# Two more feature tiles by seven products, norm 2's root begun earlier, and sums of operands moved to GpSimd

## The chip, the cores and the metric

One core of one Trainium2 chip runs the kernel. Its engines run side by side, each through its own queue in order: TensorE (PE, with PEld for its weight loads), VectorE (DVE), ScalarE (ACT), GpSimd (POOL) and SyncE (SP, which only issues transfers here). The metric is the device time of one execution in microseconds (us). The kernel before takes 871.9 us in the median of 3 runs (871.86 to 872.1). The page and the trace are of one execution of 871.7 us, whose span from the first to the last instruction is 869.9 us; the 1.8 us that lie around the span are taken as fixed.

## The reference

One layer of a decoder over 520 columns (512 positions of a prompt and 8 single samples) and 1024 features, in float32:

```python
xn = rmsnorm(x, norm1_g);  z = xn @ w_in                # pooling, recurrent, chunk branch and gates
x = x + (ga * (ya @ w_pa) + gb * (yb @ w_pb) + gc * (yc @ w_pc)) @ w_o
xn = rmsnorm(x, norm2_g)                                # norm 2
h = gelu(causal_dwconv(xn @ wg, cw, cb)) * (xn @ wu)    # 3072 features, 24 tiles of 128
x = x + h @ wd;  y = rmsnorm(x, final_norm_g)
```

All of the change but its part on constants lies in norm 2 and the three products of the gated mixer.

## The kernel before, in words

Features lie on the 128 partitions, the 520 columns along the free dimension, in two halves of 260. One "tile" of a product is 128 output features by 520 columns with 8 slices of 128 input features. Each float32 operand is split in two parts that TensorE takes: a high part (ScalarE copies and rounds it) and a low part (the difference). Each slice then costs three matmuls per half (high by high, high by low, low by high), so a plain tile of 8 slices is 48 matmuls of 128x260. Weights come by SyncE's queue as `raw` (a ring of 4), ScalarE makes `wh`, VectorE subtracts to get `wl` (`Chunk.low`), or, where `by_dma` is set, ScalarE writes the negated high part and GpSimd issues a transfer that adds the source to it (`low_by_dma`).

**Order.** Everything is written out once, in one order. `run_jobs` goes through the products; `now` counts tiles, and `after(n, fn)` runs `fn` when `now` has moved on by n tiles. So work of VectorE, ScalarE and GpSimd is interleaved with TensorE's by tile counts, and each engine's queue holds what is written in that order. An instruction that waits holds all that stands behind it on its engine.

**Stages.** After the last product of the first half, `w_o` (8 tiles, `wo_post` adds x, squares it and splits it into the operands `xg2`), the mixer's products come two tiles at a time: gate tiles m, m+1 (`wg`), two column blocks of the down product `wd` of the group of four before, then up tiles m, m+1 (`wu`), and two more blocks. Group p holds feature tiles 4p to 4p+3.

**Norm 2.** `rstd_small` sums the squares with five small matmuls (`n2p`), ScalarE takes the square root (behind the load of its table), VectorE and GpSimd build two diagonal tiles (`n2d`), and `rstd_bcast` spreads them over the partitions with four matmuls (`n2b`), two of each diagonal. Before, `g_post` calls the first behind gate tile 0 and the second behind gate tile 1. Plain tiles 0 to 3 are multiplied with the operands `xg2`, which lack the root; their results are scaled with it later (`fg_post`, `scaled`).

**Pairs.** From tile `MP` = 6 on, two tiles are made by seven products of half size (`Pair`, `run_pair`), each of 12 matmuls, instead of eight. They need seven operands `X0` to `X6`, made once by `operands()` from the four quarters of the scaled input (b11, b12, b21, b22: `rows`, 16 instructions) by sums and differences, each again as a high and a low part (`operand`). Their weights are sums of the raw weights (`Pair.sums`, four additions of 128x512 a pair) with their own high and low parts. `SEQ_PAIR` sets the order: product 0, a filler (half of a block of `wd`), products 3 and 2, the other half of that block, products 1, 4, 5, a filler, product 6, a filler. Tiles 4 and 5 (`MN` to `MP`) are plain, but on operands with the root (`plain`). `X0` is `X8` negated by GpSimd (`minus_first`).

**Rings.** Most tiles of 128x536 floats (`A(...)`) come from one ring of `NA` = 51; constants (`sts`, `wsT`, `bsb`, `wz`) have places of their own.

Of the kernel before, what the change touches and what calls it, by code (L numbers as in the profile page):

```python
# [16 lines left out]
P = 128  # L17
D = 1024
# [33 lines left out]
def trunk_kernel(ctx: ExitStack, tc: tile.TileContext, t: dict, o: dict):  # L52
# [35 lines left out]
    sts = const.tile([P, NSTATE], F32, name="sts")  # L88
    wsT = const.tile([P, 4, P], F32, name="wsT")
    bsb = const.tile([P, 4, P], F32, name="bsb")  # L90
# [11 lines left out]
    class Chunk:  # L102
# [5 lines left out]
        def load(self, parts=(0, None)):  # L108
            if not hasattr(self, "raw"):
                self.raw = wp.tile([P, self.size], F32, name="raw" + self.tag, bufs=2 if self.tag else RAW)  # L110
            q = slice(parts[0] * P, parts[1] * P if parts[1] else self.n)
            nc.sync.dma_start(self.raw[:, q], self.src[:, q])
# [271 lines left out]
    def constants():  # L384
        nc.sync.dma_start(sts, t["sts"])
        nc.sync.dma_start(wsT, t["wsT"])
        nc.sync.dma_start(bsb.rearrange("p g i -> p (g i)"), t["bs"].partition_broadcast(P))
# [245 lines left out]
    def pool_post(gi, ps):  # L633
# [178 lines left out]
    def wo_post(j, ps):  # L812
# [3 lines left out]
        st2[0] = square_add(st2[0], x1[j], f"x1q{j}")  # L816

# [9 lines left out]
    def fg_post(m, ps):  # L827
# [5 lines left out]
        if m < MN:  # L833
            v.tensor_mul(two(ext[:, 2:]), acc(ps), two(rs2[0]))
        else:
            s.activation(two(ext[:, 2:]), acc(ps), AF.Copy)
        fg_rest(m, ext)

    def fg_rest(m, ext):
# [13 lines left out]
        def scaled():  # L853
            if m < MN:
                v.tensor_mul(y, y, rs2[0])
# [11 lines left out]
    def half_rows(q):  # L867
        i, h = q
        bq[q] = [A(f"b{i}{h}_{n}") for n in range(2)]

# [23 lines left out]
    def plain(k):  # L894

        return [[two(xo[n][k % 4 // 2][e])[:, k % 2, :] for n in ((8, 7), (1, 5))[k // 4]] for e in range(2)]

    def diff(n, a, b):
        y = [A(f"d{n}{i}") for i in range(2)]
        for i in range(2):  # L900
            v.tensor_sub(y[i], a[i], b[i])
        return y

    def minus_first(i):
        hl = [A(f"X0{i}_{e}", F32R) for e in "hl"]
        for q, p in zip(hl, xo[8][i]):
            g.tensor_scalar(q, f(p), -1.0, None, op0=ALU.mult)
        xo.setdefault(0, []).append(hl)

    dd = {}  # L910

    def operands():
        for q in ((0, 0), (0, 1), (1, 0), (1, 1)):
            half_rows(q)
        steps = [lambda k=k: rows(k) for k in range(8)]
        steps += [lambda n=n, q=q: operand(n, bq[q]) for n, q in ((8, (0, 0)), (7, (0, 1)), (1, (1, 0)), (5, (1, 1)))]

        def d3():
            dd[3] = diff(3, bq[0, 0], bq[0, 1])

# [308 lines left out]
```

## Time and profile before

| | us |
|---|---|
| median of 3 runs | 871.9 |
| profiled execution, its span | 871.7, 869.9 |
| PE busy, share of the span | 856.5, 98% |
| DVE busy, share of the span | 591.3, 68% |
| ACT busy, share of the span | 444.6, 51% |
| POOL busy, share of the span | 128.1, 15% |

PE is the engine whose busy time fills the span. Matmuls are pipelined, so what one costs is read from how many start in a stretch and not from the mean of one. The mean granted TensorE clock is 0.995 of the full 2.4 GHz. Rows in order of time name the start, the length, the engine, the line of the kernel, the operation and its tiles as out<-in; in brackets stands how long the engine was idle before it, and what ended that.

### The profile page before, as it was taken

What the parts mean: (1) busy time and instruction counts of PE and PEld (TensorE: products, weight loads), DVE (VectorE), ACT (ScalarE), POOL (GpSimd) and SP (SyncE); (2) the same over time, 40 slices, a digit from 0 to 9 for tenths busy, and PEclk for the clock granted to TensorE, in tenths of its full rate; (3) what the DMA queues carried; (4) which work ended last, traced back from release to release, by engine and by line L of the source; (5) the groups of instructions that cost most, each with busy time, mean ns of one, the idle gap of its engine ahead of it and who ended that gap; (6) DMA issues with size and microseconds to landing.
All of it is one profiled execution on the core that took longest, in us unless ns stands there. A gap on an engine that the chain in (4) does not pass through costs nothing.

```text
span 869.9 us, 16887 instructions
## 1 busy us (share of the span) xinstructions
PE 856.5 (98%) x7142; PEld 852.7 (98%) x7142; DVE 591.3 (68%) x919; ACT 444.6 (51%) x652; POOL 128.1 (15%) x183
## 2 busy tenths in 40 slices
PE   8999999999999999999999999999999999999995
PEld 7999999999999999999999999999999999999994
DVE  5897989698875443135554797677777768778645
ACT  7555464578342343222335775556556556555642
POOL 0503411111100000020002114111110110111232
PEclk9999999999999999999999999999999999999997
DMA  9334233223233224342345975656545555555532
GB/s 291 130 116 128 65 100 97 75 86 95 76 94 102 76 95 121 98 158 87 122 139 168 209 165 125 157 110 150 134 111 155 135 122 146 122 151 133 145 97 99
DMA packets 36251, 108.40 MB, mean 125 GB/s; under 512 B 4152, under 2 KB 7352, under 8 KB 36152
## 3 DMA queue, kind: packets, MB, share of 16 engines
q1 hardware_dynamic: 25440, 83.08, 30.6%
q0 software_dynamic: 9216, 22.68, 14.1%
q10 hardware_dynamic: 1520, 1.57, 0.5%
q8 instruction: 56, 0.92, 0.4%
q14 instruction: 19, 0.16, 0.1%
HBM read 92.13 MB, written 15.57 MB: 124 GB/s over the span
## 4 chain that ended last, share of the span: by engine, by line
PE 97%; DVE 1%; ACT 1%; DMA 0%; SPq 0%; issue 0%; POOL 0%; DVEq 0%; POOLq 0%; ACTq 0%
PE pj L206 73%; PE pa L257 12%; PE c L257 6%; PE pf L257 3%; PE lru L206 1%; DMA x<-in_x 0%; PE vm L749 0%; PE po L206 0%; DVE bc L519 0%; DVE y L1051 0%; PE vt L742 0%; ACT L537 0%; PE n31p L452 0%; ACT n31d L461 0%; PE n30p L452 0%
## 5 line engine op out<-in xcount | busy, mean ns | idle before, releaser
L127 DVE TENSOR_TENSOR wl<-raw,wh 128x1024 fp32r<-128x1024 f32 (+1 forms) x108 | 126.4, 1176 | 36.8 <-ACT wh L118 36.7
L206 PE MATMUL pj<-xn_h,wh 128*128 128x260 f32 x704 | 141.9, 283 | 0.1
L206 PE MATMUL pj<-xn_l,wh 128*128 128x260 f32 x704 | 141.4, 282 | 0.0
L206 PE MATMUL pj<-xn_h,wl 128*128 128x260 f32 x704 | 140.8, 281 | 0.0
L118 ACT ACTIVATE wh<-raw 128x1024 fp32r<-128x1024 f32 (+1 forms) x118 | 117.7, 1005 | 4.4 <-DMA raw<-in_w_in 2.3
L206 PEld LDWEIGHTS pj<-xn_l,wh 128*128 128x128 f32 x704 | 108.7, 188 | 0.0
L206 PEld LDWEIGHTS pj<-xn_h,wh 128*128 128x128 f32 x704 | 108.1, 188 | 0.3 <-ACT r L537 0.3
L206 PEld LDWEIGHTS pj<-xn_h,wl 128*128 128x128 f32 x704 | 108.2, 188 | 0.0
L206 PE MATMUL pj<-h_l,wh 128*128 128x260 f32 x384 | 82.5, 282 | 0.6 <-DVE h_l L956 0.6
L206 PE MATMUL pj<-h_h,wh 128*128 128x260 f32 x384 | 82.4, 282 | 0.0
L206 PE MATMUL pj<-h_h,wl 128*128 128x260 f32 x384 | 82.3, 282 | 0.0
L1008 POOL DMA_DIRECT2D x1d<-dn x40 | 35.1, 877 | 263.7 <-ACT dn L1007 263.7
L206 PEld LDWEIGHTS pj<-h_l,wh 128*128 128x128 f32 x384 | 61.3, 188 | 0.8 <-DVE h_l L956 0.8
L206 PEld LDWEIGHTS pj<-h_h,wl 128*128 128x128 f32 x384 | 61.3, 188 | 0.0
L206 PEld LDWEIGHTS pj<-h_h,wh 128*128 128x128 f32 x384 | 61.1, 188 | 0.0
L690 ACT ACTIVATE gt<-pj 128x520 f32<-128x520 f32 x24 | 14.5, 606 | 81.3 <-PE pj L206 81.2
L187 DVE TENSOR_TENSOR wl<-sum,wh 128x1024 fp32r<-128x1024 f32 x36 | 43.9, 1220 | 0.9 <-ACT wh L184 0.9
L164 DVE TENSOR_TENSOR wl<-raw,wh 128x1024 fp32r<-128x1024 f32 x18 | 22.1, 1226 | 31.8 <-ACT wh L161 31.8
L184 ACT ACTIVATE wh<-sum 128x1024 fp32r<-128x1024 f32 x36 | 37.8, 1050 | 0.8 <-DVE sum L179 0.8
L848 DVE SCALAR_TENSOR_TENSOR fc<-fg,par,fc 128x512 f32<-128x512 f32 x48 | 36.0, 749 | 1.1 <-ACT fc L844 0.3
L955 ACT ACTIVATE h_h<-fc 128x520 fp32r<-128x520 f32 x24 | 15.4, 640 | 24.4 <-DVE fc L987 11.1
L1007 ACT ACTIVATE dn<-pj 128x520 f32<-128x520 f32 x40 | 23.9, 598 | 6.6 <-PE pj L206 5.0
(482 smaller groups left out, 2329.1 us busy)
## 6 DMA issues: line engine op xcount, KB each, us to landing
raw<-in_w_in SPq DMA_DIRECT2D x50, 512.0 KB, 3.6
raw<-in_wg SPq DMA_DIRECT2D x24, 512.0 KB, 4.0
raw<-in_wu SPq DMA_DIRECT2D x24, 512.0 KB, 3.9
raw<-in_wd SPq DMA_DIRECT2D x24, 512.0 KB, 5.3
x1d<-dn POOLq DMA_DIRECT2D x40, 260.0 KB, 4.4
raw<-in_w_pb SPq DMA_DIRECT2D x8, 512.0 KB, 3.6
raw<-in_w_o SPq DMA_DIRECT2D x8, 512.0 KB, 3.5
wl<-in_wu POOLq DMA_DIRECT2D x6, 512.0 KB, 8.2
```

The source lines that it names most:

```text
L118: s.activation(self.h[:, q], self.raw[:, q], AF.Copy)
L127: v.tensor_sub(self.l[:, q], self.raw[:, q], f(self.h[:, q]))
L164: v.tensor_sub(self.new("h1", "wl"), self.raw[1], f(self.W["h1", "wh"]))
L184: s.activation(self.new(n, "wh"), self.s[n], AF.Copy)
L187: v.tensor_sub(self.new(n, "wl"), self.s[n], f(self.W[n, "wh"]))
L206: te.matmul(ps[:, h, :TH], ww, xx[h] if isinstance(xx, list) else xx[:, h * TH:(h + 1) * TH], start=first and n == 0, stop=last and n == 2)
L257: te.matmul(bank[b], ww, xx, start=seen[b] + j + e == 0, stop=i >= (6, 1, 5)[b] and j == 3 and e == 2, skip_group_check=True)
L690: s.activation(two(y), acc(ps), AF.Sigmoid)
L848: v.scalar_tensor_tensor(y[:, :SEQ], ext[:, r:r + SEQ], pc("fcw", r * MF + m), y[:, :SEQ], op0=ALU.mult, op1=ALU.add)
L955: after(0.25, lambda: s.activation(h, y, AF.Copy))
L1007: s.activation(two(y), acc(ps), AF.Copy)
L1008: nc.gpsimd.dma_start(x1d[:, j, :], y, accum_op=ALU.add)
```

## The change

- `MP` goes from 6 to 4 and `MN` is gone: tiles 4 and 5 become a pair, in `wg` and in `wu`. The low parts of all eight remaining plain tiles are made by transfer (`by_dma=True`); gate tiles 0 and 1 had theirs from VectorE.
- Norm 2's sums are written 0.75 tiles, its broadcast 1.25 tiles behind the end of `w_o` (`N2`), inside gate tiles 0 and 1; gate tile 1 is then scaled as its result leaves PSUM.
- `X0` is b11 itself. `X2` is negated instead (in `operand`, `sign=-1.0`), and `add_parts`, `wg_out` and `wu_out` take the signs into account. The sums and differences for the operands and the multiplication `scaled` go from VectorE to GpSimd (`g.tensor_sub`, `g.tensor_add`, `g.tensor_mul`). The steps are 0.3 tiles apart for the first eight, then 0.4.
- `sts` becomes four loads (`h0t`, `rcs`, `ffs`, `pls`); these but `h0t`, and `wsT`, `bsb`, `wz` and the small raw weights, move into the ring, which has 57 places.

```diff
     def constants():
-        nc.sync.dma_start(sts, t["sts"])
-        nc.sync.dma_start(wsT, t["wsT"])
...
+        for d, c in ((h0t, S_H), (rcs, S_RC), (ffs, S_FF), (pls, S_PL)):
+            nc.sync.dma_start(d, t["sts"][:, c:c + d.shape[1]])
+        nc.sync.dma_start(wsT, t["wsT"].rearrange("p g i -> p (g i)"))
...
         st2[0] = square_add(st2[0], x1[j], f"x1q{j}")
+        if j == 7:
+            after(N2[0], norm2)
+            after(N2[1], norm2_rows)
...
         def scaled():
-            if m < MN:
-                v.tensor_mul(y, y, rs2[0])
+            if m < MP:
+                g.tensor_mul(y, y, rs2[0])
...
+        def first_diff():
+            d3.extend(A(f"d{i}") for i in range(2))
+            onto(g.tensor_sub, d3, b11, b12)
+
         steps = [lambda k=k: rows(k) for k in range(8)]
...
+        steps += [lambda: operand(0, b11), first_diff, lambda: operand(3, d3),
+                  lambda: onto(g.tensor_sub, b12, b22, b12), lambda: operand(1, b21),
+                  lambda: onto(g.tensor_add, d3, d3, b22), lambda: operand(5, b22), lambda: operand(2, d3, -1.0),
+                  lambda: onto(g.tensor_sub, d3, d3, b21), lambda: operand(4, b12), lambda: operand(6, d3)]
         for i, fn in enumerate(steps):
-            after(XSTEP[0] * min(i, 12) + XSTEP[1] * max(0, i - 12), fn)
+            after(XSTEP[0] * min(i, 8) + XSTEP[1] * max(0, i - 8), fn)
...
+    def norm2():
+        n2[0] = rstd_small([st2[0]], D, "n2")
+
+    def norm2_rows():
+        rs2[0] = rstd_bcast(n2[0], "n2")
+        for i in range(8):
+            if i in held:
+                x = held.pop(i)
                 v.tensor_mul(x[:, 2:], x[:, 2:], rs2[0])
                 fg_rest(i, x)
-            after(0.25, operands)
+        after(0.25, operands)
...
+    def add_parts(n, o_, a, b):
+        if n == "c12":
+            v.scalar_tensor_tensor(o_, a, -1.0, b, op0=ALU.mult, op1=ALU.subtract)
+        else:
+            v.tensor_add(o_, a, b)
...
-NA, RAW, HS, LS, LOADS, HLEAD, LLEAD = 51, 4, 6, 6, 3, 3, 2
+NA, RAW, HS, LS, LOADS, HLEAD, LLEAD = 57, 4, 6, 6, 3, 3, 2
 NP = 6
-MN, MP = 4, 6
-XSTEP = (0.4, 0.4)
+MP = 4
+N2 = (0.75, 1.25)
+XSTEP = (0.3, 0.4)
```

Over the whole program TensorE's queue holds 7105 instructions before and 7081 now, VectorE's 921 and 928.

ScalarE around norm 2's root (`n` is the small tile with the mean squares and their root, `fg` a gate tile on its way to the convolution, `n2r` the broadcast root). Before:

```order
L99 ACTIVATE wl<-wh 128x1024
L831 ACTIVATE fg_5531<-pj 128x520
L467 ACT_TABLE_LOAD
L467 ACTIVATE n_5541<-n_5540 104x5
L118 ACTIVATE wh<-raw 128x1024
L99 ACTIVATE wl<-wh 128x1024
L831 ACTIVATE fg_5612<-pj 128x520
L489 ACTIVATE n2r<-n2b 128x520
```

Now:

```order
L98 ACTIVATE wl<-wh 128x1024
L471 ACT_TABLE_LOAD
L471 ACTIVATE n_5534<-n_5533 104x5
L838 ACTIVATE fg_5561<-pj 128x520
L117 ACTIVATE wh<-raw 128x1024
L98 ACTIVATE wl<-wh 128x1024
L493 ACTIVATE n2r<-n2b 128x520
```

The table and the root stand ahead of gate tile 0's copy, and gate tile 1's copy is gone. On TensorE, 24 matmuls stand between `n2p` and `n2b` now, and 48 before.

VectorE in the two plain tiles ahead of the first product of tiles 4 and 5 (`X..l` are low parts of operands, `fc` an activated gate tile, `h_l` a low part for the down product). Before, from tile 3's scaling with the root to its product with its up tile (`fc_5843` is tile 2, `fc_5926` tile 3):

```order
L855 TENSOR_TENSOR fc_5926<-fc_5926,n2r 128x520
L950 TENSOR_TENSOR fc_5843<-pj,fc_5843 128x520
L901 TENSOR_TENSOR d_6018<-b_0_5656,b_0_5658 128x520
L901 TENSOR_TENSOR d_6019<-b_1_5657,b_1_5659 128x520
L884 TENSOR_TENSOR X50l<-b_0_5662,X50h 128x520
L884 TENSOR_TENSOR X51l<-b_1_5663,X51h 128x520
L956 TENSOR_TENSOR h_l<-fc_5843,h_h 128x520
L884 TENSOR_TENSOR X30l<-d_6018,X30h 128x520
L884 TENSOR_TENSOR X31l<-d_6019,X31h 128x520
L924 TENSOR_TENSOR d_6070<-b_0_5662,d_6018 128x520
L924 TENSOR_TENSOR d_6071<-b_1_5663,d_6019 128x520
L950 TENSOR_TENSOR fc_5926<-pj,fc_5926 128x520
```

Now, from the low part of X5 to the weights of the third product (`wl<-sum` are low parts of the pair's summed weights, the first of them for products 3 and 4, the second for products 2 and 5; `wl<-raw` is that of the filler; `fc_5872` and `fc_5946` belong to tiles 2 and 3):

```order
L887 TENSOR_TENSOR X51l<-b_1_5617,X51h 128x520
L169 TENSOR_TENSOR wlq<-raw,whq 128x512
L940 TENSOR_TENSOR fc_5872<-pj,fc_5872 128x520
L885 SCALAR_TENSOR_TENSOR X20l<-d_5826,X20h 128x520
L885 SCALAR_TENSOR_TENSOR X21l<-d_5827,X21h 128x520
L186 TENSOR_TENSOR wl<-sum,wh 128x1024
L126 TENSOR_TENSOR wl<-raw,wh 128x1024
L946 TENSOR_TENSOR h_l<-fc_5872,h_h 128x520
L887 TENSOR_TENSOR X40l<-b_0_5612,X40h 128x520
L887 TENSOR_TENSOR X41l<-b_1_5613,X41h 128x520
L940 TENSOR_TENSOR fc_5946<-pj,fc_5946 128x520
L186 TENSOR_TENSOR wl<-sum,wh 128x1024
```

The sums for the operands have left this queue, and the low parts of the pair's weights have come into it.

GpSimd in the same two tiles. Before:

```order
L829 MEMSET fg_5923 128x2
L100 DMA wl<-in_wg 128x1024
L100 DMA wl<-in_wu 128x1024
L829 MEMSET fg_6157 128x2
L100 DMA wl<-in_wu 128x1024
L829 MEMSET fg_6239 128x2
L907 TENSOR_SCALAR X_h<-X80h 128x520
L907 TENSOR_SCALAR X_l<-X80l 128x520
```

Now:

```order
L836 MEMSET fg_5869 128x2
L899 TENSOR_TENSOR b_0_5612<-b_0_5616,b_0_5612 128x520
L899 TENSOR_TENSOR b_1_5613<-b_1_5617,b_1_5613 128x520
L859 TENSOR_TENSOR fc_5872<-fc_5872,n2r 128x520
L836 MEMSET fg_5943 128x2
L899 TENSOR_TENSOR d_5826<-d_5826,b_0_5616 128x520
L899 TENSOR_TENSOR d_5827<-d_5827,b_1_5617 128x520
L859 TENSOR_TENSOR fc_5946<-fc_5946,n2r 128x520
L899 TENSOR_TENSOR d_5826<-d_5826,b_0_5614 128x520
L899 TENSOR_TENSOR d_5827<-d_5827,b_1_5615 128x520
```

Transfers of low parts and the negations have gone, and instructions of 128x520 that read two tiles have come.

## Rows read from the trace of the kernel before

**Rows 1.** The page, busy time of each engine over the whole span

```profile
PE 856.5 (98%) x7142; PEld 852.7 (98%) x7142; DVE 591.3 (68%) x919; ACT 444.6 (51%) x652; POOL 128.1 (15%) x183
```

**Rows 2.** Busy time in stretches: PE, PEld, DVE, ACT, POOL, then clock, DMA

```profile
428.00:480.00 52.00, 52.00 (x438) 52.00 (x438) 25.45 (x36) 23.29 (x31) 7.79 (x13) 1.00 0.51 155
480.00:520.00 40.00, 40.00 (x337) 40.00 (x336) 34.91 (x67) 29.80 (x40) 5.54 (x9) 1.00 0.82 179
...
550.00:700.00 150.00, 150.00 (x1254) 150.00 (x1253) 109.36 (x172) 86.02 (x137) 17.16 (x29) 1.00 0.55 130
```

**Rows 3.** The chain of waits: start, length, engine, line, count

```profile
30.45 5.86 PE pj L206 x48
...
236.07 235.49 PE pj L206 x1968
472.38 5.87 PE pj L206 x48
478.74 68.89 PE pj L206 x576
```

**Rows 4.** VectorE in order of time (start, length, instruction), end of norm 2's root

```profile
473.75 0.19 DVE L469 RECIPROCAL n2h<-n 104x5 fp32r<-104x5 f32 x1 [1.17 <-ACT n L467]
...
475.54 0.70 DVE L463 TENSOR_TENSOR n2d<-ident,n2l 104x520 fp32r<-104x520 f32 x1
```

**Rows 5.** ScalarE in order of time, around norm 2's root

```profile
469.76 1.06 ACT L99 ACTIVATE wl<-wh 128x1024 fp32r<-128x1024 f32 x1
...
472.21 1.28 ACT L467 ACT_TABLE_LOAD   x1
473.51 0.21 ACT L467 ACTIVATE n<-n 104x5 f32<-104x5 f32 x1
```

**Rows 6.** VectorE in order of time, before and at the first pair

```profile
515.26 0.69 DVE L950 TENSOR_TENSOR fc<-pj,fc 128x520 f32<-128x520 f32 x1
515.87 1.22 DVE L127 TENSOR_TENSOR wl<-raw,wh 128x1024 fp32r<-128x1024 f32 x1
517.01 0.70 DVE L956 TENSOR_TENSOR h_l<-fc,h_h 128x520 fp32r<-128x520 f32 x1
...
520.52 1.54 DVE L848 SCALAR_TENSOR_TENSOR fc<-fg,par,fc 128x512 f32<-128x512 f32 x2 [0.29 <-ACT fc L844]
...
522.12 0.69 DVE L884 TENSOR_TENSOR X40l<-d,X40h 128x520 fp32r<-128x520 f32 x1
...
523.34 1.30 DVE L901 TENSOR_TENSOR d<-b,d 128x520 f32<-128x520 f32 x2
...
536.80 0.68 DVE L176 TENSOR_TENSOR sum<-raw 128x512 f32<-128x512 f32 x1
...
540.47 0.69 DVE L956 TENSOR_TENSOR h_l<-fc,h_h 128x520 fp32r<-128x520 f32 x1
```

**Rows 7.** GpSimd in order of time, two stretches

```profile
86.19 2.53 POOL L650 TENSOR_TENSOR ps<-ps 128x524 f32<-128x524 f32 x2
...
474.02 1.06 POOL L463 TENSOR_TENSOR n2d<-ident,n2h 104x520 fp32r<-104x520 f32 x1 [1.89 <-DVE n2h L469]
```

**Rows 8.** VectorE in order of time, beside GpSimd's work and without it

```profile
86.26 1.56 DVE L658 SCALAR_TENSOR_TENSOR pd<-ps,a 128x512 f32<-128x512 f32 x1
87.85 0.90 DVE L659 TENSOR_TENSOR pd<-ps,rc 128x3 f32<-128x3 f32 x1
...
109.73 0.69 DVE L658 SCALAR_TENSOR_TENSOR pd<-ps,a 128x512 f32<-128x512 f32 x1
110.45 0.17 DVE L659 TENSOR_TENSOR pd<-ps,rc 128x15 f32<-128x15 f32 x1
```

**Rows 9.** SyncE's queue in order of time, a load of constants

```profile
14.11 0.43 SPq L385 DMA_DIRECT2D sts<-in_sts  x1
```

**Rows 10.** VectorE in order of time, the end of norm 1's root

```profile
34.77 0.70 DVE L463 TENSOR_TENSOR n1d<-ident,n1l 104x520 fp32r<-104x520 f32 x1 [0.54 <-DVE n1l L474]
```

More of the change, by code (lines that the diff above doesn't have):

```diff
@@ L87, in trunk_kernel @@
     nc.scalar.dma_start(par, t["par"])
-    sts = const.tile([P, NSTATE], F32, name="sts")
-    wsT = const.tile([P, 4, P], F32, name="wsT")
-    bsb = const.tile([P, 4, P], F32, name="bsb")
+    h0t = const.tile([P, S_RC - S_H], F32, name="h0t")
+    early = {}
     def pc(n, i=0, m=1):
@@ L109, in load @@
             if not hasattr(self, "raw"):
-                self.raw = wp.tile([P, self.size], F32, name="raw" + self.tag, bufs=2 if self.tag else RAW)
+                self.raw = A("rawq", w=self.size) if self.tag else wp.tile([P, self.size], F32, name="raw", bufs=RAW)
             q = slice(parts[0] * P, parts[1] * P if parts[1] else self.n)
@@ L892, in op_of, with onto @@
         return get
[L894 to L899, printed above, removed]
+    def onto(fn, o_, a, b):
         for i in range(2):
[L901 to L908, printed above, removed]
@@ new lines, in operands @@
+    def operands():
+        b11, b12, b21, b22 = (bq.setdefault(q, [A(f"b{q[0]}{q[1]}_{n}") for n in range(2)])
+                              for q in ((0, 0), (0, 1), (1, 0), (1, 1)))
+        d3 = []
+        def first_diff():
+            d3.extend(A(f"d{i}") for i in range(2))
+            onto(g.tensor_sub, d3, b11, b12)
+        steps = [lambda k=k: rows(k) for k in range(8)]
+        steps += [lambda: operand(0, b11), first_diff, lambda: operand(3, d3),
+                  lambda: onto(g.tensor_sub, b12, b22, b12), lambda: operand(1, b21),
+                  lambda: onto(g.tensor_add, d3, d3, b22), lambda: operand(5, b22), lambda: operand(2, d3, -1.0),
+                  lambda: onto(g.tensor_sub, d3, d3, b21), lambda: operand(4, b12), lambda: operand(6, d3)]
@@ L930, in operands @@
         for i, fn in enumerate(steps):
-            after(XSTEP[0] * min(i, 12) + XSTEP[1] * max(0, i - 12), fn)
+            after(XSTEP[0] * min(i, 8) + XSTEP[1] * max(0, i - 8), fn)
     def g_post(m, ps):
         ext = fg_post(m, ps)
-        if m == 0:
-            held[0] = ext
-            n2[0] = rstd_small([st2[0]], D, "n2")
-        elif m == 1:
-            rs2[0] = rstd_bcast(n2[0], "n2")
-            for i, x in enumerate((held.pop(0), ext)):
+        if ext is not None:
+            held[m] = ext
@@ L1100, in trunk_kernel @@
     s.activation(warm, ones, AF.Exp)
-    wz = const.tile([P, 512], BF16, name="wz")
+    wz = ap_.tile([P, 536], F32, name="wz", tag="a", bufs=NA)[:, :256].bitcast(BF16)
     v.memset(wz, 0.0)
```

62 lines of the change are left out of this document (25 added, 37 removed).

## The prediction

> **What bounds the kernel now.** I read the page's busy times first: PE is busy in 98% of the span, no other engine above 68% [rows 1]. A mean over the span says little of one stage, so the table by stretches came next: from 428 to 520 us and from 550 to 700 PE is busy in every microsecond, while DVE, the next one, has 34.91 of 40 us from 480 to 520, where the operands for the pairs are made, and 109.36 of 150 in the pairs [rows 2]. Then the chain of waits: its pieces in this part are PE alone, one of 576 matmuls in 68.89 us [rows 3]. So PE's queue sets the end: a matmul less is its time less, and a result that comes late is a stall that nothing hides. DVE, at 87% from 480 to 520, is the engine that may be late.
>
> Prices from the chain [rows 3]: 68.89 / 576 = 0.1196 us a matmul; the pairs have 1254 in 150 us, the same [rows 2]. A plain tile of 48 is 5.74 us, a product or filler of 12 is 1.44. One piece ends at 236.07 + 235.49 = 471.56, the next starts at 472.38: 0.82 for the five `n2p`. That ends at 478.25, the next starts at 478.74: 0.49 for the four `n2b`.
>
> **Term 1, the pairs.** Two gate and two up tiles cost 4 x 48 = 192 matmuls as plain tiles, and 2 x 7 x 12 = 168 as two pairs. 24 fewer, as the counts of the queue say: 24 x 0.1196 = 2.87 us less.
>
> **Term 2, norm 2's root.** Before, PE finds the broadcast's inputs ready: the sums end at 472.38, the second diagonal at 475.54 + 0.70 = 476.24, so the root takes 3.86 us, and PE comes for it at 478.25 [rows 3, 4]. Now only 24 matmuls lie between. Gate tile 0 starts at 471.56 - 5.74 = 465.82, the sums stand behind 36 matmuls (4.31) and end at 465.82 + 4.31 + 0.82 = 470.95. PE comes to the second diagonal 24 matmuls and half a broadcast later: 470.95 + 2.87 + 0.24 = 474.06. The root: ScalarE ends its last weight copy at 469.76 + 1.06 = 470.82, loads the table until 472.10, and takes the root; from root to reciprocal are 0.24 us, from there to the end of the second diagonal 476.24 - 473.75 = 2.49 [rows 4, 5]. That is 474.85. PE waits 0.8 us. Bounds: 0, if the table came earlier (then the root takes 3.86 less the 0.9 that it waited for its table), and 1.8, if one more weight copy of 1.06 comes late ahead of the table. Below zero it can't go, as PE has no wait here before. I take 0.8. Behind the broadcast stands all of gate tile 1, so the wait shifts everything.
>
> **Term 3, the first pair.** Call G the time at which PE ends gate tile 3, T the time at which it ends up tile 3, two tiles later (T = G + 11.48). At G, DVE must wait for tile 3's result, whatever it has done by then, so its queue can be summed from G on. Step costs are start to start [rows 6]: a product from PSUM 515.87 - 515.26 = 0.61; a low part of 128x520 (523.34 - 522.12) / 2 = 0.61; the convolution of a tile 522.12 - 520.52 = 1.60; low weights of 128x1024 517.01 - 515.87 = 1.14; the four sums of a pair with its first low weights 540.47 - 536.80 = 3.67. The queue: tile 3's product and a small copy 0.8; the sums and the first low weights 3.67; convolution 1.60; X5's low parts 1.22; the half-size low weights 0.6; tile 2's product 0.61; X2's low parts, now with three operands, 1.4; summed weights h2 1.14; filler weights 1.14. That ends at G + 12.2. PE wants the filler's low weights in the filler after product 0, four matmuls in: T + 1.44 + 0.48 = G + 13.4. Then h2's low part 0.61, X4's 1.22, tile 3's product 0.61 and the summed weights h3 1.14 end at G + 15.8, and product 2, third in order, wants those at T + 3 x 1.44 + 0.24 = G + 16.0. So with nothing in its way DVE is in time, by 0.2 to 1.2 us.
>
> But five GpSimd instructions of 128x520 that read two tiles start in this stretch: the addition of b22 (two), tile 3's scaling, the subtraction of b21 (two). The trace shows what such an instruction does to DVE. Beside two of them, 2.53 us long [rows 7], a DVE instruction took 1.56 us that takes 0.69 alone, and one of a few columns 0.90 for 0.17 [rows 8]: 0.87 and 0.73 lost, 0.8 for each. The first of the five starts beside tile 3's product, which DVE reads from PSUM; I count half for it, and 4.5 x 0.8 = 3.6 in all. Less the 0.2 of room, PE waits 3.4 us: 2.4 in the filler, the rest at product 2. Bounds: 0, if they fall where DVE waits or reads one tile, and 5.1, if each holds DVE for all its 1.06 us [rows 7]. I take 3.4, from the nearest rows: the same engines and kinds of instruction. The second pair's weights come 15.8 us later, with no such GpSimd work, and DVE has 27% to spare in the pairs [rows 2], so it catches up.
>
> The Trainium skill (SBUF — State Buffer, Who interferes with whom) says that a VectorE instruction with two SBUF inputs and a GpSimd instruction that reads SBUF share a port, and the later one "fully blocks". The trace agrees in kind, with 0.8 us of a length of 1.06 to 1.27; the rule alone would give the upper bound, a rival below. The Trainium skill also advises against GpSimd for elementwise work on tiles (GPSIMD Engine Reference, Engine selection): an addition costs DVE 0.61 us when it does it, and loses it 0.8 when GpSimd does it beside it, so here the advice holds wherever DVE is busy.
>
> **At nothing.** Low parts of gate tiles 0 and 1 by transfer: 2 x 1.14 off DVE and 2 x 1.06 onto ACT, which has 23.29 of 52 us busy there, and two more transfers on POOL (7.79 of 52) [rows 2]; uncovered, they would cost PE some 1 us each. Sums on GpSimd ahead of G: they hold DVE too, but DVE waits for PE's gate tiles 2 and 3 there. Changed signs in the pairs: two instructions a pair take another form; DVE has the room. X0 without its negation: it is first wanted at T, its rows are done five tiles earlier. Six loads of constants for three: SyncE issues each in 0.43 us [rows 9], so norm 1's first diagonal on GpSimd comes 1.3 us later; the second ended at 34.77 + 0.70 = 35.47 [rows 10], and PE came for both at 30.45 + 5.86 = 36.31 [rows 3]. 0.8 of room; uncovered, 0.5 us. The last load of `w_o` stands behind one of `wg` now, three tiles ahead of its use. The ring gains six places for seven long-lived tiles: as many free as before once these are done.
>
> **Sum.** -2.87 + 0.8 + 3.4 = +1.3 us on the 871.7 us of the profiled execution, which stands 0.2 below the median: 873.2 us at a median of 871.9. About 0.2% (1.7 us) is what a measurement of this kernel tells from no change, and the forecast lies inside it.
>
> **Rivals.** (B) DVE is in time: GpSimd's five instructions fall into DVE's gaps, or DVE's are served first. For it: DVE has the room of its wait at G, and 0.2 to 1.2 us of room need no more than one hold. Against it: [rows 8], where GpSimd got its turn beside a full DVE queue. Only terms 1 and 2 are left: -2.1, 869.8; with no wait for the root either, 869.0. (C) Each of the five holds DVE for its whole length: 5 x 1.06 = 5.3, less 0.2, so -2.87 + 0.8 + 5.1 = +3.0, 874.9, slower; it decides from about 0.9 us of hold for each. The section of the Trainium skill named above (SBUF — State Buffer) says this, "for the whole instruction"; against it stand the 0.73 and 0.87 of [rows 8]. (D) The root alone costs more: with a late weight copy 1.8, and 874.2 with term 3. (E) The change doesn't do what it says, and the pairs' 24 matmuls are not saved: the counts exclude it.
>
> **Chances.** Forecast 0.40 (872.3 to 874.2, as the holds come to 2.5 to 4.4 us); B 0.34; C and D together 0.18; a part of the holds, 871 to 872, 0.08. Faster by over 0.2%: most of B, 0.27. Slower by over 0.2% (873.6): C and D, and a third of the forecast, 0.31. Within: 0.42. The range goes from 869.3, where B is nearly whole, to 875.0, C's time; as cases of both signs hold it, the forecast's own range stands beside it: 872.3 to 874.2.
>
> **What would show it.** Term 1: 24 fewer matmuls, no change of 0.1196. Term 2: one PE wait of about 0.8 us at `n2b`, ended by VectorE's second diagonal. Term 3: PE waits of 2 to 4 us in all on `wl` from DVE in the filler after the first product 0 and at product 2, and DVE instructions of 1.4 us in place of 0.6 beside GpSimd's. Wrong, if PE runs through there, if DVE's lengths don't change, or if the second pair waits as well.

## The result and the profile after

The changed kernel takes 878.25 us (four executions, 877.75 to 879.25) against 872.0 before: 1.0073 times as long, with a 95% interval of 1.0061 to 1.0086. Five more executions, in a later experiment, gave 878.49. The prediction was 873.2, between 869.3 and 875.0. The kernel is slower, as forecast, but by 6.3 us where 1.3 were forecast, and the time lies outside the range. The trace below is of the execution of 879.25 us (span 877.5).

TensorE's waits, after (engine, line, what it waited for: us in total, times, longest):

```profile
PE pj L205 <- DVE wl L126: 5.2, 1, 5.2
...
PE n2b L488 <- DVE n2d L467: 0.7, 1, 0.7
```

Neither stands in the trace before. The second is term 2, forecast at 0.8. The first is term 3, forecast at 3.4 in two places; it came in one, the filler after product 0. Its mechanism is the forecast one, VectorE's lateness at the first pair's weights. Busy time after, in the stretches of [rows 2] and in two short ones behind the wait (PE, PEld, DVE, ACT, POOL, granted clock, DMA share, GB/s):

```profile
428.00:480.00 52.00, 51.34 (x430) 51.03 (x429) 24.89 (x37) 27.64 (x36) 10.07 (x16) 1.00 0.63 176
480.00:520.00 40.00, 37.92 (x317) 37.71 (x315) 37.20 (x56) 24.31 (x35) 20.40 (x17) 1.00 0.51 132
515.00:523.00 8.00, 2.92 (x25) 2.71 (x23) 8.00 (x9) 4.77 (x8) 3.89 (x2) 0.96 0.39 128
523.00:530.00 7.00, 6.92 (x34) 6.93 (x35) 6.97 (x12) 1.05 (x3) 0.00 (x0) 0.55 0.26 77
...
550.00:700.00 150.00, 150.00 (x1254) 150.00 (x1253) 112.31 (x177) 87.60 (x138) 16.21 (x28) 1.00 0.56 139
```

The last row is, for TensorE, the one of [rows 2]: 1254 matmuls in 150 us. From 515 to 523 VectorE is busy all 8 us and TensorE 2.92. Then comes what no term had: from 523 to 530 TensorE is busy all the time and does 34 matmuls where [rows 2] would have 58. The granted clock is 0.55 there, that is mostly 1.2 GHz in place of 2.4, behind an idle time of 5.15 us. The chain of waits shows it (start, length, instruction, count):

```profile
520.73 2.30 DVE wl L126
523.03 0.04 issue
523.08 2.10 PE pj L205 x8
525.18 2.60 PE c L256 x12
527.78 2.16 PE pa L256 x12
```

32 matmuls in 6.86 us; at 0.1196 each they are 3.83, so 3.0 us more. The Trainium skill (TensorE: Matmul & The Clock Gate, Part 1) says that an idle TensorE falls to half its clock; this trace agrees.

Why is VectorE late? Its instructions after, in order of time (start, length, instruction); at 505.16 it takes gate tile 3's result (L840):

```profile
499.93 1.89 DVE L887 TENSOR_TENSOR X30l<-d,X30h 128x520 fp32r<-128x520 f32 x1
...
505.16 0.69 DVE L840 TENSOR_TENSOR fg<-pj,n2r 128x520 f32<-128x520 f32 x1
505.88 0.61 DVE L847 COPY small<-fg 128x10 f32<-128x10 f32 x1
...
507.08 1.69 DVE L176 TENSOR_TENSOR sum<-sum,raw 128x512 f32<-128x512 f32 x1
508.69 1.79 DVE L178 TENSOR_TENSOR sum<-raw 128x512 f32<-128x512 f32 x1
...
513.72 1.82 DVE L887 TENSOR_TENSOR X50l<-b,X50h 128x520 fp32r<-128x520 f32 x1
...
518.51 2.30 DVE L186 TENSOR_TENSOR wl<-sum,wh 128x1024 fp32r<-128x1024 f32 x1
520.73 2.29 DVE L126 TENSOR_TENSOR wl<-raw,wh 128x1024 fp32r<-128x1024 f32 x1
```

And GpSimd's, beside them:

```profile
498.69 2.57 POOL L899 TENSOR_TENSOR b<-b,b 128x520 f32<-128x520 f32 x2
...
504.77 1.66 POOL L859 TENSOR_TENSOR fc<-fc,n2r 128x520 f32<-128x520 f32 x1 [3.51 <-ACT fc L863]
...
506.41 3.52 POOL L899 TENSOR_TENSOR d<-d,b 128x520 f32<-128x520 f32 x2
512.82 2.17 POOL L859 TENSOR_TENSOR fc<-fc,n2r 128x520 f32<-128x520 f32 x1 [2.89 <-ACT fc L863]
518.05 3.89 POOL L899 TENSOR_TENSOR d<-d,b 128x520 f32<-128x520 f32 x2 [3.07 <-DVE X20l L885]
```

From 504.77 on there are six GpSimd instructions, and six of VectorE's are too long; what one loses beside a GpSimd instruction is called a hold here. Without company they take 0.17, 0.69, 0.68, 0.69, 1.21 and 1.21 us (from other places of this trace and the one without sums, below). So 0.44, 1.00, 1.11, 1.13, 1.09 and 1.08 are lost, 5.85 in all; five of the six holds are as long as GpSimd's own 1.06 [rows 7]. GpSimd's six grow too, to 1.66 to 2.17 us each.

A last difference can't be seen in any wait. Norm 1's broadcast and norm 2's sums, after:

```profile
36.65 0.65 PE L488 MATMUL n1b<-n1d,onesr 104*128 104x260 f32 x4
...
471.62 0.99 PE L456 MATMUL n2p<-ones,x1q 128*104 128x1 f32 x10
```

From one to the other are 434.97 us. Before, [rows 3] give 236.07 + 235.49 - (30.45 + 5.86) = 435.25; but there 12 matmuls (1.43 us) more stand between, as the sums came behind all of gate tile 0. So the same work takes 1.15 us more, with TensorE busy throughout in both.

**The balance.** -2.87 (24 matmuls) + 0.7 (root) + 1.15 (spacing) + 5.15 (wait) + 3.0 (half clock) = +7.1; measured on this execution, spans of 877.5 and 869.9: +7.6, of which 0.5 lies ahead of norm 1's broadcast; the second tile of the input reached ScalarE 0.4 us later (6.88 for 6.44).

### The profile page after: what moved, and what is told of

The parts are those of the page before. It is cut to its first block, busy times and chain, and to the rows that moved or that the text cites. A ratio compares the mean times of both kernels' runs of the same rounds, so it can differ in the third digit from the quotient of the medians.

```text
span 877.5 us, 16859 instructions
## 1 busy us (share of the span) xinstructions
PE 858.6 (98%) x7118; PEld 854.4 (97%) x7118; DVE 602.9 (69%) x926; ACT 445.5 (51%) x658; POOL 139.6 (16%) x189
## 4 chain that ended last, share of the span: by engine, by line
PE 93%; DVE 4%; ACT 1%; issue 1%; DMA 1%; SPq 0%; POOL 0%; DVEq 0%; ACTq 0%; POOLq 0%
PE pj L205 67%; PE pa L256 13%; PE c L256 7%; PE pf L256 3%; PE lru L205 1%; DMA x<-in_x 1%; PE vm L753 0%; PE po L205 0%; DVE wl L126 0%; DVE bc L523 0%; DVE fc L852 0%; DVE y L1047 0%; ACT wl L98 0%; DVE X30l L887 0%; DVE sum L178 0%
## 5 line engine op out<-in xcount | busy, mean ns | idle before, releaser
L126 DVE TENSOR_TENSOR wl<-raw,wh 128x1024 fp32r<-128x1024 f32 (+1 forms) x106 | 124.7, 1182 | 35.2 <-ACT wh L117 35.2
L117 ACT ACTIVATE wh<-raw 128x1024 fp32r<-128x1024 f32 (+1 forms) x114 | 113.5, 1004 | 4.4 <-DMA raw<-in_w_in 2.3
L186 DVE TENSOR_TENSOR wl<-sum,wh 128x1024 fp32r<-128x1024 f32 x40 | 49.8, 1245 | 0.0
L163 DVE TENSOR_TENSOR wl<-raw,wh 128x1024 fp32r<-128x1024 f32 x20 | 24.5, 1225 | 31.0 <-ACT wh L160 31.0
L183 ACT ACTIVATE wh<-sum 128x1024 fp32r<-128x1024 f32 x40 | 42.0, 1050 | 0.0
L260 ACT ACTIVATE m<-pa 128x260 f32<-128x260 f32 x40 | 15.3, 383 | 22.8 <-PE pa L256 22.7
```

Of the source, the lines that this page charges most:

```text
L117: s.activation(self.h[:, q], self.raw[:, q], AF.Copy)
L126: v.tensor_sub(self.l[:, q], self.raw[:, q], f(self.h[:, q]))
L163: v.tensor_sub(self.new("h1", "wl"), self.raw[1], f(self.W["h1", "wh"]))
L183: s.activation(self.new(n, "wh"), self.s[n], AF.Copy)
L186: v.tensor_sub(self.new(n, "wl"), self.s[n], f(self.W[n, "wh"]))
L260: s.activation(kept["AFC"[b] + str(seen[b])], bank[b], AF.Copy)
```

## Experiments

The first theory: GpSimd's instructions hold VectorE for their whole length, VectorE is late, TensorE idles for 5 us and then runs at half clock. The rivals: VectorE has too much work of its own; the slow matmuls are slow for another reason. All times are medians beside runs of the kernel before on the same chip (871.9 to 872.0).

**1. The sums left out.**

```diff
-            d3.extend(A(f"d{i}") for i in range(2))
-            onto(g.tensor_sub, d3, b11, b12)
+            d3.extend(b11)
...
-                  lambda: onto(g.tensor_sub, b12, b22, b12), lambda: operand(1, b21),
+                  lambda: None, lambda: operand(1, b21),
...
```

The addition of b22 and the subtraction of b21 go in the same way.

> The changed kernel with the GpSimd sums of the operand blocks left out (the pairs then work on the blocks themselves, so what they compute is no longer the product; every other instruction stays, on its engine). Theory (holds and a cold clock): the eight GpSimd instructions make VectorE late, which costs a wait of 5.15 us in the first filler and, as TensorE then runs at half clock, 3.0 us more. Without them VectorE loses the time of one or two scalings at the most, so the wait falls to 0 to 0.7 us, the clock stays at 1.00 and the time comes to 878.2 - 5.15 - 3.0 = 870.1 us (869.5 to 871.5). Rival (VectorE simply has too much work of its own in this stretch): the wait stays at 4 us or more and the time above 876.

872.56 us, ratio 1.0007 (0.9998 to 1.0016). VectorE there:

```profile
504.19 0.70 DVE L840 TENSOR_TENSOR fg<-pj,n2r 128x520 f32<-128x520 f32 x1 [0.83 <-PE pj L205]
...
506.34 0.68 DVE L178 TENSOR_TENSOR sum<-raw 128x512 f32<-128x512 f32 x1
...
510.26 1.82 DVE L887 TENSOR_TENSOR X50l<-b,X50h 128x520 fp32r<-128x520 f32 x1
...
516.18 1.21 DVE L126 TENSOR_TENSOR wl<-raw,wh 128x1024 fp32r<-128x1024 f32 x1
```

L178 takes 0.68 again for 1.79, L126 1.21 for 2.29; X50's low part, beside the one scaling that is left, still 1.82. VectorE waits for gate tile 3 (0.83 us) instead of being late for it. The filler's low weights end at 517.39, 13.2 us behind the start of L840; take the one hold of 1.13 off and it is 12.1, where the prediction's count of the queue says 12.2. The 5.15 and the half clock are gone, as the theory says, and 0.7 us of wait come at h3's low weights (the second summed weights, which product 2 wants), the upper end of what was expected. The time is 2.5 above the expected 870.1, outside its range: 0.7 is this wait, and up to 1.2 comes from the half clock, which cost 1.8 us and not 3.0 in another execution (experiment 4); 0.6 or more stay open.

**2. The sums on VectorE.**

```diff
-            onto(g.tensor_sub, d3, b11, b12)
+            onto(v.tensor_sub, d3, b11, b12)
...
```

The other three sums likewise.

> The changed kernel with the eight sums of 128x520 on VectorE in place of GpSimd. Theory (holds): each costs VectorE its own 0.61 us instead of a hold of about 1.0, six of them behind tile 2's work, so about 2.4 of the 5.15 us come back: a wait of 2.7 us, and 875.8 us if the clock still falls behind it, 872.8 if it does not. Rival (GpSimd's instructions cost VectorE nothing, its own work is too much): 6 x 0.61 = 3.7 us more, a wait near 8.8 and 882 us.

875.05 us. TensorE's waits:

```profile
PE pj L205 <- DVE wl L126: 3.0, 1, 3.0
...
PE pa L256 <- DVE wl L186: 0.7, 1, 0.7
```

3.0 where the theory had 2.7 and the rival 8.8. The work moved onto VectorE and VectorE got faster. Behind 3.0 us of idling the clock did not fall (granted 1.00 from 515 to 530). For that case the expectation said 872.8; 0.3 of longer wait, the 0.7 at h3 and 1.2 for a half clock of 1.8 us in place of 3.0 (experiment 4) make it 875.0.

**3. Dummy matmuls in the wait.**

```diff
+                if n == first_pair and i == 0:
+                    for _ in range(DUMMY):
+                        te.matmul(fps[i][:, 0, :TH], c.w(0, a)[0], get(0)[0][:, :TH], start=True, stop=True)
...
+DUMMY = 40
```

> The changed kernel with 40 matmuls of 128x260 added in the first filler, ahead of its own, into the same accumulator (overwritten afterwards, so the result is the same): 40 x 0.1196 = 4.8 us of work in the place where TensorE waits 5.15. Theory (cold clock): the wait falls to about 0.4 us, the granted clock stays at 1.00 behind it, and the 32 matmuls that took 6.86 us take 3.83: 878.2 - 3.0 = 875.2 us, faster with more work. Rival (these matmuls are slow for another reason, such as late weights or traffic): the same 878.2 us, and still 0.2 us for each of them.

877.27 us: 1.0 less with 4.8 us more work. The stretch behind the wait, and the waits:

```profile
523.00:530.00 7.00, 6.33 (x52) 6.12 (x52) 6.97 (x12) 3.00 (x6) 0.00 (x0) 1.00 0.26 75
```

```profile
PE pa L257 <- DVE wl L186: 0.7, 1, 0.7
...
PE pj L205 <- DVE wl L126: 0.4, 1, 0.4
```

The clock is 1.00 where it was 0.55, so the slow matmuls came from idling. But 2.0 of the 3.0 us did not come back. 0.7 is clear: at full speed TensorE comes to h3's low weights before VectorE has them. The rest needed experiment 4.

**4. The changed kernel again.** Nothing edited.

> The changed kernel once more, unaltered, beside the versions below. Its four executions lay 1.5 us apart, and the one in the profile was the slowest. Theory: the wait of 5.15 us, the half clock of 6.8 us behind it and the 1.15 us of the slower spacing are the same in every execution, and what differs is when the first input lands: 878.2 us median (877.5 to 879), first weights' wait at 5.1 to 5.2. Rival (the half clock comes in some executions only, so that the dummies could give back only 1.0 us): a trace with the clock at 1.00 behind the wait, or with a low stretch of another length.

878.49 us (877.72 to 878.77). The wait is 5.1 again, but the low stretch is shorter:

```profile
523.00:530.00 7.00, 7.00 (x49) 7.00 (x49) 6.96 (x12) 2.72 (x5) 0.00 (x0) 0.79 0.23 77
```

```profile
522.56 2.10 PE pj L205 x8
524.66 2.06 PE c L256 x12
526.73 1.44 PE pa L256 x12
```

20 matmuls in 4.16 us against 2.39: 1.8 lost, not 3.0. So the rival is right in one part: the half clock came in both traces, for unequal times. Of the 1.7 us between their spans (877.5 and 875.8) 1.2 are this, and 0.45 lie ahead of norm 1's broadcast, as the theory has it (36.65 and 36.20). With 1.8 to 3.0 for the half clock the balance gives +5.9 to +7.1; the medians say +6.25 and +6.5. The dummies' 1.0 us fits as 1.8 less the 0.7 at h3.

**5. The filler's low weights by transfer.**

```diff
-                for dt, fn in ((-2.25, c.load), (-0.75, c.high), (-0.5, c.low)):
+                c.by_dma = n == min(pairs)
+                for dt, fn in ((-2.75, c.load), (-1.75, c.high), (-1.5, c.low)) if c.by_dma else ((-2.25, c.load), (-0.75, c.high), (-0.5, c.low)):
```

> The changed kernel with the first filler's low weights made as those of the plain tiles are (a negated copy on ScalarE and a transfer that adds), loaded, copied and issued 0.5, 1.0 and 1.0 tiles earlier. Theory (VectorE's queue is late, and its last instruction there is this one): 1.14 us of work and about 1.1 of hold leave VectorE's queue; what PE meets then is the summed weights h3, done near 520.8 where product 2 wants them near 520.4, so a wait of 0 to 0.8 us, no fall of the clock, and 878.2 - 5.15 - 3.0 + 0.4 = 870.5 us (869.8 to 871.5). Rival (the wait is for something else, or the transfer is late behind GpSimd's sums): a wait of 2 us or more, and 873 us or more.

877.96 us: a miss. The waits and the stretch:

```profile
PE pa L256 <- DVE wl L186: 2.1, 1, 2.1
...
PE c L256 <- DVE wl L186: 1.6, 1, 1.6
```

```profile
523.00:530.00 7.00, 4.93 (x29) 4.77 (x28) 6.97 (x11) 2.57 (x5) 0.00 (x0) 0.76 0.01 2
```

Between the two, 0.6 us went on a copy of ScalarE. I had taken the low weights at 518.51 for h3's; they are h2's, and h3's come later. One instruction less at the end of a late queue shows the next late one.

**6. Pairs from tile 6 again**, all else as changed.

```diff
-MP = 4
+MP = 6
```

> The changed kernel with pairs from feature tile 6 on, as before the change; norm 2's root, GpSimd's sums, the operands' signs and the memory part stay. Theory (GpSimd's holds cost only because the first pair comes two tiles of each kind earlier): VectorE has 23 us more, no wait in the first filler, clock at 1.00; what is left is the root's 0.7 and the 1.15 of the slower spacing: 871.9 + 0.7 + 1.15 = 873.8 us (873.2 to 874.4). Rival (the sums on GpSimd make the first pair late wherever it stands): a wait of 2 us or more there and 877 us or more.

874.62 us, no wait on VectorE at the first pair; 0.5 us on a transfer of low weights (`wl<-in_wu`) and the root's 0.7. With 1.15 + 0.7 + 0.5 on 872.0 it is 874.35. With two tiles of each kind more ahead of the first pair, the same GpSimd sums make no wait there.

**7 to 9. Spacing.** First the memory part alone on the kernel before: of the change, the hunks of `h0t`, `early`, `rawq`, `wz` and `constants()`, and the ring's size. Then an unused constant ahead of all others in the kernel before. Then the first again with a ring of 56. One line of each:

```diff
-NA, RAW, HS, LS, LOADS, HLEAD, LLEAD = 51, 4, 6, 6, 3, 3, 2
+NA, RAW, HS, LS, LOADS, HLEAD, LLEAD = 57, 4, 6, 6, 3, 3, 2
```

```diff
+    pad = const.tile([P, 32], F32, name="pad")
     par = const.tile([P, NPAR], F32, name="par")
```

```diff
-NA, RAW, HS, LS, LOADS, HLEAD, LLEAD = 57, 4, 6, 6, 3, 3, 2
+NA, RAW, HS, LS, LOADS, HLEAD, LLEAD = 56, 4, 6, 6, 3, 3, 2
```

> The kernel before with the memory part of the change alone: constants of early stages, the half-size raw weights and the warm-up tile in the ring, ring of 57, six loads for three; no work on any engine is changed. In the trace of the changed kernel the stretch from norm 1's broadcast to norm 2's sums took 434.97 us in each of five traces of it or its variants, and 435.25 before, with 12 matmuls (1.43 us) fewer ahead of the sums: 1.15 us that no term of the prediction has. Theory M (the memory part does it): 436.4 us here for the 435.25, and 873.0 us in all. Rival (it comes from the moved norm 2 or the pairs): 435.25 and 871.9 us.

> The kernel before with one unused constant of 128 bytes a partition ahead of all others, so that every tile stands 128 bytes further on; nothing else differs. Theory A (where tiles stand sets the spacing of matmuls): the stretch from norm 1's broadcast to norm 2's sums differs from 435.25 us by 0.2 us or more, in either direction, and the time with it. Rival (the spacing does not hang on places; then what M finds comes from the constants' loads or tiles in the ring): 435.25 within 0.05, 871.9 us.

> The kernel before with the memory part alone and a ring of 56 in place of 57. Theory A (places): the stretch of 436.42 us differs by 0.2 us or more. Rival (constants in the ring): 436.42 within 0.05.

The two rows of the memory part alone, and of the ring of 56:

```profile
36.76 0.65 PE L488 MATMUL n1b<-n1d,onesr 104*128 104x260 f32 x4
...
473.19 0.99 PE L456 MATMUL n2p<-ones,x1q 128*104 128x1 f32 x10
```

```profile
36.34 0.65 PE L488 MATMUL n1b<-n1d,onesr 104*128 104x260 f32 x4
...
473.24 0.99 PE L456 MATMUL n2p<-ones,x1q 128*104 128x1 f32 x10
```

436.43 and 436.90, for 435.25 with the ring of 51. The memory part alone takes 873.43 us (1.0017, 1.0008 to 1.0027): the 1.15 us are its own, and its cost over the whole kernel is 1.4. The ring of 56 was executed once (874.26 us). The 128 bytes changed nothing (435.25, and 871.71 us).

**10. Three transfers and the sums on VectorE.** The edit of 2, the scaling on VectorE, the edit of 5, the first pair's first low weights by transfer, X5 behind X4, and:

```diff
-                    for lead, fn in zip((4, 3, 2.9) if c.by_dma else (3, 2, 1.5), (c.load, c.high, c.low)):
+                    for lead, fn in zip((4, 2.2, 2.1) if c.by_dma else (3, 2, 1.5), (c.load, c.high, c.low)):
...
-            v.tensor_sub(self.new("h1", "wl"), self.raw[1], f(self.W["h1", "wh"]))
+            if self.early:
+                low_by_dma(self.new("h1", "wl"), self.W["h1", "wh"], self.src[1])
...
```

> The changed kernel with less on VectorE and none of GpSimd's tile work ahead of the first pair: the sums and the scaling on VectorE (875.05 us measured for the sums), the first filler's low weights and the first pair's first low weights by transfer (1.14 us each off VectorE), X5 made behind X4 (1.22 us later wanted), and the plain tiles' copies 0.8 tiles later, so that none stands ahead of norm 2's root on ScalarE. Theory: of the waits of that kernel (3.0 us for the filler's weights, 0.7 for h3's low weights, 0.7 for the root) none is left: 875.05 - 4.4 = 870.6 us (869.9 to 871.8), faster than before. Rival (transfers or ScalarE become late in turn): a wait of over 1.5 us on a transfer or on ScalarE, and 872 us or more.

876.15 us. The root's wait is gone, but the rival came:

```profile
PE pa L260 <- DMA wl<-in_wg: 3.1, 1, 3.1
PE pj L209 <- DMA wl<-in_wd: 1.9, 1, 1.9
```

ScalarE waited 2.66 us for a result of VectorE with the negated copies queued behind it, so the transfers were issued at 510.75 and 512.22 and came late. What leaves a late engine still waits for it through a second one.

**11 to 13. The operands in the order of their use.** X1, X5, X4 and X6 and their sums behind the start of the first pair; first alone, then with sums and scaling on VectorE and the leads of 10, then with a ring of 56.

```diff
-        steps += [lambda: operand(0, b11), first_diff, lambda: operand(3, d3),
...
+        later_steps = ((3.9, lambda: operand(0, b11)), (4.3, first_diff), (4.7, lambda: operand(3, d3)),
+                       (5.1, lambda: onto(g.tensor_add, d3, d3, b22)), (5.5, lambda: operand(2, d3, -1.0)), (8.0, lambda: operand(1, b21)),
+                       (8.3, lambda: onto(g.tensor_sub, b12, b22, b12)), (8.5, lambda: operand(4, b12)), (8.35, lambda: operand(5, b22)),
+                       (8.9, lambda: onto(g.tensor_sub, d3, d3, b21)), (9.1, lambda: operand(6, d3)))
...
+        for at_, fn in later_steps:
+            after(at_ - 1.5, fn)
```

The numbers are tiles after the end of `w_o`; the first pair starts at 8.

> The changed kernel with the operands' steps in the order in which the pair's products want them, and X1, X5, X4, X6 with their sums put behind the start of the first pair; all sums stay on GpSimd, nothing is added or left out. Theory (VectorE is late at the first pair, through its own low parts and GpSimd's holds together): X5's low parts (1.2 us), X1's (1.2) and the holds of four to six GpSimd instructions leave the stretch ahead of the filler, so the wait of 5.15 us falls to 0 to 1 us, the clock stays at 1.00 and the time comes to 872.0 us (871.3 to 873.3): 878.2 less 5.15 and the 1.0 that the dummy matmuls gave back, and the operands that come later are still in time. Rival (what is moved is missed later: X1, X4, X5 or X6 make the products of the first pair wait as much): 875 us or more, with waits of 3 us or more inside the pair.

> The same order, with the sums and the scaling on VectorE in place of GpSimd and the plain tiles' copies 0.8 tiles later (none ahead of norm 2's root). Theory: VectorE's queue counted from the end of gate tile 3 ends the filler's low weights 3 us and h3's 2 us before TensorE wants them, so no wait is left at the first pair, and none for the root; against the kernel without sums (872.56) 0.7 us for h3 and 0.9 for the root go: 870.9 us (870.2 to 871.9), faster than before by 0.1%. Rival (the sums on VectorE, 0.61 us each, make it late all the same): a wait of 1.5 us or more and over 872.4 us.

> The kernel of the run before with a ring of 56 in place of 57. Theory A (which place a tile has sets the spacing of matmuls): the stretch from norm 1's broadcast to norm 2's sums is not 434.97 us but differs by 0.2 us or more, and the time by as much or more, in either direction. Rival (constants in the ring cost the time, whatever the size): 434.97 within 0.05, and the same time.

The order alone: 874.51 us; of the 5.15 a wait of 0.5 is left, and 2.1 in three places behind it (1.1 of it for h3, 0.5 in the second pair). With the sums on VectorE: 872.91 us, nothing at the filler, nothing at h3, nothing at the root, but

```profile
PE pa L256 <- DVE X60l L887: 1.1, 1, 1.1
...
PE pa L256 <- ACT m L260: 0.5, 1, 0.5
...
PE pa L256 <- DVE X40l L887: 0.4, 1, 0.4
```

so 2 us above the expected 870.9. The ring of 56: 873.5 us, the stretch 0.50 longer (435.47), as in 9 (0.47).

**14 to 16. X4 and X6 earlier, a ring of 54, a pad of 32 bytes.**

```diff
-                       (8.3, lambda: onto(v.tensor_sub, b12, b22, b12)), (8.5, lambda: operand(4, b12)), (8.35, lambda: operand(5, b22)),
-                       (8.9, lambda: onto(v.tensor_sub, d3, d3, b21)), (9.1, lambda: operand(6, d3)))
+                       (8.2, lambda: onto(v.tensor_sub, b12, b22, b12)), (8.22, lambda: operand(4, b12)), (8.4, lambda: operand(5, b22)),
+                       (8.7, lambda: onto(v.tensor_sub, d3, d3, b21)), (8.71, lambda: operand(6, d3, 1.0, 0.2)))
```

The second and third are this kernel with `NA` = 54, and with the pad of 7 to 9 at 8 floats in place of 32.

> The reordered kernel with all sums on VectorE, where the trace showed 0.4 us of wait for X4's low parts and 1.1 for X6's in the first pair: X4's difference goes ahead of h3's low weights (which were 1.6 us early), X4 ahead of X5, and X6 ahead of half of the next pair's sums. Theory: both waits go and nothing else comes: 872.9 - 1.5 = 871.4 us (871.0 to 872.0), slightly faster than before, and as fast as terms 1 and 2 and the spacing leave it. Rival (VectorE has no time left in the first pair, so the wait moves): a new wait of 1 us or more, on h3's weights, on X5 or in the second pair, and 872.5 us or more.

> The same kernel with a ring of 54 in place of 57. Theory A (places set the spacing): the stretch from norm 1's broadcast to norm 2's sums is not 434.97 us; ring 51 gave 1.17 less and 56 gave 0.5 more, so a change between -1.2 and +0.7 us, and the time of the kernel by as much. Rival (a shorter ring makes an engine wait for a free place): waits that the kernel with 57 does not have, and a time above it by more than the stretch.

> The same kernel (ring of 57) with an unused constant of 32 bytes a partition ahead of all others: every tile stands 32 bytes further on, none changes its place against another. Theory A1 (only the order of tiles in the ring counts, as 128 bytes further on changed nothing in the kernel before): the stretch stays at 434.97 us within 0.05. Rival A2 (a tile's start against a boundary of 64 bytes counts): it differs by 0.2 us or more.

873.05 us: the waits for X4 and X6 went and 2.2 us came in two places where ScalarE copies an accumulator (`m`), behind copies that wait for VectorE: 0.7 in the first pair behind X6's, 1.5 in the second behind those of gate tiles. The rival was right. The ring of 54:

```profile
36.77 0.65 PE L488 MATMUL n1b<-n1d,onesr 104*128 104x260 f32 x4
...
470.31 0.99 PE L456 MATMUL n2p<-ones,x1q 128*104 128x1 f32 x10
```

433.54, 1.43 less than with 57, and 872.36 us, which is only 0.7 less. The rest went behind that stretch. The two rows from which this is read, up to the sums of the final norm, are with 57 and with 54:

```profile
471.70 0.99 PE L456 MATMUL n2p<-ones,x1q 128*104 128x1 f32 x10
...
859.76 1.19 PE L456 MATMUL n31p<-ones,x2q 128*65 128x1 f32 x16 [0.42 <-POOL x2q L1025]
```

```profile
859.37 1.12 PE L456 MATMUL n31p<-ones,x2q 128*65 128x1 f32 x16 [0.49 <-POOL x2q L1025]
```

388.06 and 859.37 - 470.31 = 389.06: 1.0 more with 54, of which 0.2 are waits. The pad of 32 bytes: 434.97 as without it, 873.21 us. So the number of places in the ring changes the spacing, in either direction; 32 or 128 bytes more ahead of everything do nothing. How the 1.15 us divide between six more places and the constants that now stand in the ring is not shown.

**17. A version that beats both.** Ring of 54, X6's copies on ScalarE behind the accumulator's, and the second pair's first low weights and its filler's by transfer, early enough.

```diff
-                       (8.7, lambda: onto(v.tensor_sub, d3, d3, b21)), (8.71, lambda: operand(6, d3, 1.0, 0.2)))
+                       (8.7, lambda: onto(v.tensor_sub, d3, d3, b21)), (8.85, lambda: operand(6, d3, 1.0, -0.05)))
...
+            self.early = len(pairs) == 1
...
-            return ((-15, self.load), (-8, lambda: self.sums(0)), (-7, lambda: self.sums(1)), (-7, self.high1),
-                    (-6, lambda: self.sums(2)), (-6, self.low1), (-6, self.high0), (-5, self.low0),
+            return ((-15, self.load), (-8, lambda: self.sums(0)), (-7, lambda: self.sums(1)), (-8 if self.early else -7, self.high1),
+                    (-6, lambda: self.sums(2)), (-7.7 if self.early else -6, self.low1), (-6, self.high0), (-5, self.low0),
...
+                c.by_dma = n == sorted(pairs)[1]
+                for dt, fn in ((-2.75, c.load), (-1.97, c.high), (-1.91, c.low)) if c.by_dma else ((-2.25, c.load), (-0.75, c.high), (-0.5, c.low)):
```

> The reordered kernel with ring 54, and what its trace asked for: X6's copies on ScalarE behind the accumulator's copy that product 4 waits for (0.9 us of wait in the first pair), and the second pair's first low weights and its filler's low weights by transfer, 1.14 us each off VectorE, whose lateness kept a second copy of an accumulator waiting (1.5 us). Theory: both waits go and the transfers land in time: 872.36 - 2.4 = 870.0 us (869.5 to 870.9), faster than before by 0.2%. Rival (a transfer is late, as two were in the version with three transfers): a wait of 1 us or more on a transfer and 871.5 us or more.

870.29 us, 0.9982 (0.9973 to 0.9991) of the kernel before, within the expected range. In the pairs TensorE's list of waits has one left:

```profile
PE c L260 <- DVE X50l L892: 0.3, 1, 0.3
```

## Why the prediction was wrong

**Term 1 was right.** 24 matmuls fewer at an unchanged price [rows 2].

**Term 2 was right**: 0.7 for 0.8. That copies on ScalarE ahead of the table made it is borne out by 10 and 12 to 17: with those copies later no wait is left there.

**Term 3 failed in three places; its queue did not.** Without GpSimd's sums the queue came out within 0.1 us of the count (12.1 for 12.2).
- "At G, DVE must wait for tile 3's result, whatever it has done by then": it did not wait. TensorE ended gate tile 3 at 515.83 - 11.48 = 504.35 (product 0 starts at 515.83), and VectorE came to it at 505.16. Its room of 0.83 (experiment 1) was used up, and 0.8 more, by the sums ahead of G: beside the one at 498.69 X30's low part took 1.89 us there for 0.69. With that falls "Sums on GpSimd ahead of G: they hold DVE too, but DVE waits for PE's gate tiles 2 and 3 there", costed at nothing.
- "0.87 and 0.73 lost, 0.8 for each", for five GpSimd instructions and 3.6 in all: six did hold VectorE, as tile 2's scaling came behind G too, five of them for 1.00 to 1.13, 5.85 in all. I took the nearest rows [rows 8] and not the bound of 1.06 [rows 7]. The Trainium skill (SBUF — State Buffer, Who interferes with whom) had said "for the whole instruction", and here the trace agrees: 1.00 to 1.13 us for an instruction of 1.06.
- A term was missing: what TensorE loses behind a long wait. I summed the wait and went on at 0.1196 a matmul. It cost 1.8 to 3.0 us.

Together: 12.2 + 0.8 + 5.85 = 18.9 us behind G, wanted at 13.4: 5.5, for a measured 5.15. The time came out 5.0 us above the forecast: 1.75 is this wait beyond 3.4, 1.8 to 3.0 the half clock behind it, and 1.15 the spacing below.

**"At nothing" was wrong for the ring.** I counted free places, and the loads, which were rightly nothing (no wait at norm 1's broadcast). That the number of places changes the spacing of matmuls I had not in mind: 1.15 us with the memory part, shown by 7 to 9, 13 and 15.

**The rivals.** C named the mechanism and the point ("from about 0.9 us of hold for each"), and with D it had only 0.18 of the chances, but its 874.9 had neither the lateness at G, nor the half clock, nor the spacing. B fell, and so did D (0.7 at the root).

What stays open is why the count of places acts on the spacing, and how a wait turns into a low stretch of one length or another.

## What to carry to other kernels

Beside a full VectorE queue count each GpSimd instruction that reads two tiles at its whole length, from the last point at which VectorE is seen to wait, and check that it will still wait there. Moving an operation off the late engine can cost it more than it saves (a hold of 1.0 to 1.1 us for 0.61 of work); putting the operands in the order of their use was worth more (3.7 us). A wait of TensorE of some 5 us is to be priced with what follows it, and a change of a pool's size is measured alone, over the whole kernel, before it rides along with something else.

## What was not expected of the hardware

- The same matmuls, all back to back at a granted clock of 1.00, took 435.25 us with a ring of 51 places, 436.43 with 57 and 436.90 with 56; with the moved sums 433.54 with 54, 434.97 with 57 and 435.47 with 56. Twelve traces with a ring of 57 and the moved sums agree within 0.02 us, so it is no noise. What one stretch gains another can lose (1.43 and 1.0 us with 54).
- TensorE kept its full clock behind one wait of 3.0 us (2), and in 10, where it was busy 3.08 of the 8 us from 515 to 523; it fell to half in 5, with waits of 1.6, 0.6 and 2.1 us close together, and behind 5.15 us of idling (after, 4).
- A VectorE copy of ten columns was held as well: 0.61 us for 0.17.
